# A hybrid diffusion backbone on one core: lent load buffers are taken until the first phase's last load, and the build pictures transfers at 405 GB/s

## The chip, the core and the metric

The kernel runs on one core of a Trainium2 chip. A core has four engines that compute: TensorE (PE in the profile, its weight loads PEld), VectorE (DVE), ScalarE (ACT) and GpSimd (POOL). Each works through its own list of instructions in order, and waits on semaphores for the others. A fifth, SyncE (SP), here only issues transfers (DMA) from the chip's memory (HBM); these transfers, once issued, share 16 DMA engines. The metric is the time of one execution on the device, in microseconds (us).

## The reference, cut to what matters

One trunk layer (D_MODEL 2048) is computed for 128 context tokens and for 128 latent tokens with the same weights; the kernel puts both side by side as 256 columns. Each kind of token has its own shift and scale from a conditioning vector. What the first phase of the kernel covers is the start of `block`:

```python
def block(x, mod, p, lb, s0_hg, s0_gdn, rows):
    shift1, scale1, gate1, shift2, scale2, gate2 = jnp.split(mod, 6, axis=-1)   # mod = silu(c) @ w_mod + b_mod
    h = rmsnorm(x, p['norm1_g']) * (1.0 + scale1) + shift1
    (hq, hi, hgo, hff, hfb, cu, cv, gqkv, ggo, ga, gbeta, gates) = jnp.split(h @ p['w_in'], ...)
    o_a, s_hg = hgrn2_branch(...)        # three branches over the columns of h @ w_in
    o_b = chunk_mlp_branch(...)
    o_c, s_gdn = gdn_branch(...)
    merged = g_a * (o_a @ p['w_br_hg']) + g_b * (o_b @ p['w_br_cm']) + g_c * (o_c @ p['w_br_gdn'])
    x = x + gate1 * (merged @ p['w_out'])
    h2 = rmsnorm(x, p['norm2_g']) * (1.0 + scale2) + shift2
    x = x + gate2 * (jnp.square(jax.nn.relu(h2 @ p['w_ff1'])) @ p['w_ff2'])
```

All arrays are float32. Weights are read once, and nearly all of the 460 MB that move are weights.

## The kernel before, in words

**Units and steps.** The weights come in units of 128 x 1024 float32 (512 KB). `run_stream` (line 393) gets a list of steps, most of them one unit with its matmuls, and emits instructions for all engines while it walks along the list. A normal unit is split first (`split`, line 388): ACT casts it to a rounded copy `wh`, DVE computes the remainder `wl` (a subtraction), and PE then runs three products for each piece (high by high, high by low, low by high), 24 matmuls for a unit in the first phase. A "whole" unit is not split: PE multiplies it as it is.

**The first phase.** It has 88 units, numbered 0 to 87 here. 64 of them are whole: the columns of `w_mod` for shift1 and scale1 (`in_wmods`), eight for each of eight blocks of 256 columns, chain 0 to chain 7. After the eighth unit of a block a short chain of work (`chain` in `start_steps`) turns the sum into shift and scale and applies them to two of the 16 row blocks of h: ACT copies the sum (`m<-pf`), PE transposes it (`pf<-sel,m`), DVE adds the bias (`modc`, `gs`) and scales (`tp`), ACT modulates (`tp<-tp,modc,gs`, four times) and casts (`Hh`), DVE computes `Hl`. The other 24 units are normal ones of `w_in` (`in_win`, `in_winh`), of the forget gates, and are woven in between: the three that use chain n's rows come when chain n is done. At the end stand units 81 and 82 (the last of `w_mod`), 83 (the transposes of chain 7 lie in the middle of its matmuls), 84, and then 85, 86 and 87, which need chain 7. Unit 88 is the first of the second phase, from where all units are normal.

**Load buffers.** Three buffers of one unit (`raw`) serve the whole program. In the first phase twelve more are lent: the halves of six large tiles (`z`) that the program needs only later. SP issues a load when a buffer is free, in the order of the units: a whole unit frees its buffer when PE has multiplied it, a normal one when DVE has subtracted. In `run_stream` a lent buffer is taken up again only while fewer than `last` loads have been issued; before, `last` is `self.lend - len(raws)`, that is 88 - 15 = 73. So loads 0 to 72 may go to any of 15 buffers, later ones to three. The split copies have three pairs of buffers, and two further lent pairs (`z` again) while fewer than 88 loads have been issued.

**The order is written by the build.** Every engine's list comes from a planning clock in the build (`Clock`, `Meter`): each instruction that is emitted is booked at an estimated time. The side work of a phase (chains, normalisations, scans) is written as generators, "fillers"; `pump` lets a filler emit its next piece when by that clock its inputs are ready and DVE and ACT are not ahead by more than a margin. `run_stream` decides in the same way how early a unit is split: not if by that clock its load lands more than 1.5 us after PE's present time. Transfers are booked one behind the other at a fixed rate, 3.6e5 bytes/us (360 GB/s). From the second phase on DVE also computes the remaining columns of `w_mod` as background work (`mods`), with loads of its own (`mraw`).

## Time and profile before

| what | value |
|---|---|
| time, median of 3 runs | 2002.61 us (2000.73 to 2003.5) |
| profiled execution: its time, its span | 2000.7 us, 1998.9 us |
| mean granted TensorE clock | 0.99 |
| PE busy | 1941.3 us, 97% of the span |
| DVE, ACT busy | 1407.2 us (70%), 952.6 us (48%) |
| moved by DMA | 460.51 MB, mean 230 GB/s |
| first matmul of unit 88 | 174.65 us after the span's start |

The span goes from the first to the last instruction; the time has 1.8 us more around it. Matmuls overlap in their pipeline, so a busy PE may still run slowly: how long a unit takes is read from the start of its first matmul to the start of the next unit's. The three products of a normal unit appear as `pb<-Hh,wh`, `pb<-Hh,wl` and `pb<-Hl,wh` (with `z` in place of `wh` and `wl` where the pair of buffers is a lent one); the whole units appear as `pf<-raw,cst` or `pf<-z,cst`, by their load buffer. Line L173 is the helper through which all instructions go, so lines tell nothing and the tiles tell all.

### The profile page before, as it was taken

How to read it: one execution, taken by the hardware profiler on the slowest of the kernel's cores; microseconds unless marked ns; L12 is line 12 of the kernel's file. 1: busy time of each engine (PE TensorE's matmuls, PEld its weight loads, DVE VectorE, ACT ScalarE, POOL GpSimd, SP SyncE). 2: the span in 40 equal slices, each digit the busy share in tenths (PEclk: the TensorE clock that was granted, in tenths of full speed). 3: DMA queues.
4: the chain of work that ended last, by engine and by line, in shares of the span. 5: the costliest groups of instructions: out<-in, count | busy, mean ns of one | idle time of the engine just before them, and what ended most of it. 6: DMA issues, size and time to landing. Idle time of an engine off the chain costs nothing.

```text
span 1998.9 us, 30561 instructions
## 1 busy us (share of the span) xinstructions
PE 1941.3 (97%) x11927; PEld 1707.3 (85%) x11927; DVE 1407.2 (70%) x2064; ACT 952.6 (48%) x1419; POOL 49.0 (2%) x120
## 2 busy tenths in 40 slices
PE   6979999999999999999999999899999999999997
PEld 3758988999888889888887888899988998998886
DVE  2325898989887998856876896766766766555476
ACT  3324646476655545366543445544444443344334
POOL 0000000000000001011000000000000000000000
PEclk9999999999999999999999999999999999999999
DMA  9956667565656866756678786566667666566664
GB/s 374 403 205 225 224 209 248 188 231 190 210 186 230 269 221 228 271 176 202 234 237 308 246 282 211 182 220 225 228 225 250 218 235 230 189 203 210 210 233 148
DMA packets 125216, 460.51 MB, mean 230 GB/s; under 512 B 14416, under 2 KB 14992, under 8 KB 122896
## 3 DMA queue, kind: packets, MB, share of 16 engines
q1 hardware_dynamic: 117072, 423.96, 62.6%
q0 software_dynamic: 7568, 34.35, 5.0%
q8 instruction: 93, 1.52, 0.3%
q14 instruction: 51, 0.42, 0.1%
q10 hardware_dynamic: 432, 0.26, 0.0%
HBM read 447.97 MB, written 10.53 MB: 229 GB/s over the span
## 4 chain that ended last, share of the span: by engine, by line
PE 89%; DMA 4%; DVE 3%; ACT 2%; issue 1%; POOL 0%; ACTq 0%; POOLq 0%; DVEq 0%
PE pb L173 80%; PE pf L173 9%; DVE wl L173 1%; DMA raw<-in_win 1%; DVE z L173 1%; ACT wh L173 1%; DMA raw<-in_wff2c 1%; DMA par<-in_par 1%; DMA z<-in_win 1%; DVE m L173 0%; ACT tp L173 0%; DMA z<-in_wmods 0%; ACT z L173 0%; DMA z<-sp 0%; DMA z<-in_s0gd 0%
## 5 line engine op out<-in xcount | busy, mean ns | idle before, releaser
L173 DVE TENSOR_TENSOR wl<-raw,wh 128x1024 fp32r<-128x1024 f32 x586 | 712.3, 1220 | 442.1 <-ACT wh L173 440.5
L173 ACT CAST wh<-raw 128x1024 fp32r<-128x1024 f32 x586 | 612.5, 1048 | 801.3 <-PE pb L173 677.0
L173 PE MATMUL pb<-Hh,wh 128*128 128x256 f32 (+1 forms) x1856 | 529.1, 288 | 9.3 <-ACT wh L173 8.4
L173 PE MATMUL pb<-Hh,wl 128*128 128x256 f32 (+1 forms) x1856 | 525.5, 286 | 4.3 <-DVE wl L173 4.3
L173 PE MATMUL pb<-Hl,wh 128*128 128x256 f32 (+1 forms) x1856 | 510.7, 285 | 0.0
L173 PE MATMUL pb<-wh,z 128*128 128x512 f32 x1368 | 428.2, 392 | 0.0
L173 PEld LDWEIGHTS pb<-Hh,wh 128*128 128x128 f32 (+1 forms) x1856 | 358.8, 193 | 20.5 <-ACT wh L173 11.3
L173 PEld LDWEIGHTS pb<-Hh,wl 128*128 128x128 f32 (+1 forms) x1856 | 359.0, 193 | 6.3 <-DVE wl L173 6.0
L173 PEld LDWEIGHTS pb<-Hl,wh 128*128 128x128 f32 (+1 forms) x1856 | 350.0, 193 | 0.1
L173 PE MATMUL pb<-wh,Hh 128*128 128x512 f32 (+1 forms) x800 | 315.7, 395 | 0.1
L173 DVE SCALAR_TENSOR_TENSOR junk<-mraw,cb 128x1024 bf16<-128x1024 f32 x256 | 312.0, 1219 | 3.1 <-DMA cb<-csd 1.8
L173 PE MATMUL pb<-wl,Hh 128*128 128x512 f32 (+1 forms) x800 | 306.2, 383 | 1.4 <-DVE wl L173 1.4
L173 PE MATMUL pb<-wh,Hl 128*128 128x512 f32 (+1 forms) x800 | 306.2, 383 | 0.0
L173 PEld LDWEIGHTS pb<-wh,z 128*128 128x128 f32 x1368 | 257.6, 188 | 55.7 <-ACT z L173 0.2
L173 PE MATMUL pb<-wl,z 128*128 128x512 f32 x684 | 268.8, 393 | 2.0 <-DVE wl L173 2.0
L173 PEld LDWEIGHTS pb<-wh,Hl 128*128 128x128 f32 x800 | 151.0, 189 | 29.8
L173 PEld LDWEIGHTS pb<-wl,Hh 128*128 128x128 f32 x800 | 151.4, 189 | 28.1 <-DVE wl L173 2.4
L173 PEld LDWEIGHTS pb<-wh,Hh 128*128 128x128 f32 x800 | 151.3, 189 | 27.4 <-ACT wh L173 0.5
L173 PEld LDWEIGHTS pb<-wl,z 128*128 128x128 f32 x684 | 128.4, 188 | 32.2 <-DVE wl L173 4.1
L173 DVE TENSOR_TENSOR z<-z,z 128x512 f32<-128x512 f32 (+4 forms) x101 | 71.7, 743 | 13.3 <-ACT z L173 12.5
L173 DVE SCALAR_TENSOR_TENSOR cy<-z,par,cy 128x258 f32<-128x258 f32 (+1 forms) x192 | 53.6, 331 | 1.9
L173 PEld LDWEIGHTS pf<-m,z 128*128 128x128 f32 x384 | 49.1, 191 | 3.3 <-ACT z L173 0.4
(189 smaller groups left out, 1276.3 us busy)
## 6 DMA issues: line engine op xcount, KB each, us to landing
raw<-in_win SPq DMA_DIRECT2D x246, 512.0 KB, 4.2
raw<-in_wff SPq DMA_DIRECT2D x224, 512.0 KB, 3.8
mraw<-in_wmodr SPq DMA_DIRECT2D x128, 512.0 KB, 4.8
raw<-in_wbr SPq DMA_DIRECT2D x48, 512.0 KB, 3.8
z<-in_wmods SPq DMA_DIRECT2D x44, 512.0 KB, 10.0
raw<-in_wmods SPq DMA_DIRECT2D x20, 512.0 KB, 7.9
cb<-csd POOLq DMA_DIRECT2D x8, 1024.0 KB, 7.7
raw<-in_wouta SPq DMA_DIRECT2D x16, 512.0 KB, 4.4
```

Of the source, the lines that this page charges most:

```text
L173: return f(*a, **k)
```

## The change

Two edits. A lent buffer is now taken up again as long as fewer than 88 loads have been issued, that is until the last load of the first phase. And the planning clock books a transfer at 4.05e5 bytes/us.

```diff
@@ in Meter.__getattr__, the booking of a transfer
                 size = int(np.prod(outs[0].shape)) * 4
-                clock.dma = max(clock.dma, start + DMA0) + size / 3.6e5
+                clock.dma = max(clock.dma, start + DMA0) + size / 4.05e5
                 clock.mark("dma", rd, wr, clock.dma + DMA1)
@@ in run_stream
         lent = [self.slot(z, [P, 2, NB]) for z in (3, 4, 5, 6, 7, 0)]
         raws = [0, 1, 2] + [t[:, h, :] for t in lent for h in range(2)]
-        last = self.lend - len(raws)
+        last = self.lend
         pairs = [None] * 3 + [8, 9]
```

The work is the same: PE, DVE, POOL and SP have the same number of instructions, ACT two table loads fewer. What moves is the order, and which buffer a load goes to. Three places are shown.

SP's loads from unit 72 on, before (`z_11` to `z_16` are the six lent tiles, each `raw` one of the three standing buffers, `mraw` the first two loads of the background work):

```order
L173 DMA z_16_138<-in_win 128x1024
L173 DMA raw_800<-in_wmods 128x1024
L173 DMA raw_804<-in_wmods 128x1024
L173 DMA raw_859<-in_wmods 128x1024
L173 DMA mraw_891<-in_wmodr 128x1024
L173 DMA mraw_893<-in_wmodr 128x1024
L173 DMA raw_989<-in_winh 128x1024
L173 DMA raw_993<-in_wmods 128x1024
L173 DMA raw_997<-in_wmods 128x1024
L173 DMA raw_1004<-in_wmods 128x1024
L173 DMA raw_1032<-in_win 128x1024
```

and the same place now:

```order
L173 DMA z_16_138<-in_win 128x1024
L173 DMA z_16_138<-in_wmods 128x1024
L173 DMA z_14_136<-in_wmods 128x1024
L173 DMA raw_802<-in_wmods 128x1024
L173 DMA raw_806<-in_winh 128x1024
L173 DMA z_12_134<-in_wmods 128x1024
L173 DMA z_11_133<-in_wmods 128x1024
L173 DMA mraw_861<-in_wmodr 128x1024
L173 DMA mraw_863<-in_wmodr 128x1024
L173 DMA raw_875<-in_wmods 128x1024
L173 DMA z_12_134<-in_win 128x1024
```

Behind unit 72 the loads before went to the three standing buffers in turn; now four of the next seven go to lent ones, and the load of unit 76 (`in_winh`), which stood behind both background loads, stands ahead of them. Units 80 to 87 now all have lent buffers.

ACT's list about chain 5, before (the casts of units 61 and 65, `z_81` and `z_86`, and of unit 69, `wh_865`; `m_84`, `tp_832` and `Hh` are the chain):

```order
L173 CAST z_81_769<-z_16_138 128x1024
L173 COPY m_84_806<-pf_718 96x512
L173 ACTIVATE tp_832<-tp_832,modc,gs 128x128 x4
L173 CAST Hh_191<-tp_832 128x512
L173 CAST z_86_845<-z_12_134 128x1024
L173 COPY tp_851<-pf_849 32x128
L173 CAST wh_865<-z_14_136 128x1024
```

and now (unit 65 is `z_85`, unit 69 `wh_881`):

```order
L173 CAST z_81_769<-z_16_138 128x1024
L173 COPY m_84_808<-pf_718 96x512
L173 CAST z_85_810<-z_12_134 128x1024
L173 COPY tp_849<-pf_847 32x128
L173 ACTIVATE tp_838<-tp_838,modc,gs 128x128 x4
L173 CAST Hh_194<-tp_838 128x512
L173 ACT_TABLE_LOAD
L173 ACTIVATE rshd_870<-rshd_870 128x16
L173 CAST wh_881<-z_14_136 128x1024
```

The cast of unit 65 has moved from behind the chain's modulation to ahead of it, and DVE's subtraction with it.

ACT's list at the end of the first phase, before (the casts of units 76, 80 and 83, then chain 7, then units 84, 85 and 86):

```order
L173 CAST wh_1000<-raw_989 128x1024
L173 CAST z_113_1042<-raw_1032 128x1024
L173 CAST z_115_1071<-raw_1045 128x1024
L173 COPY m_119_1084<-pf_986 96x512
L173 ACTIVATE tp_1104<-tp_1104,modc,gs 128x128 x4
L173 CAST Hh_191<-tp_1104 128x512
L173 CAST wh_1123<-raw_1074 128x1024
L173 CAST wh_1129<-raw_1078 128x1024
L173 CAST wh_1160<-raw_1082 128x1024
```

and now (unit 76 has moved up ahead of chain 6's modulation; then units 80, 83, 84, 85, 86, chain 7, and unit 87):

```order
L173 CAST wh_961<-raw_806 128x1024
L173 ACTIVATE tp_991<-tp_991,modc,gs 128x128 x4
L173 CAST Hh_194<-tp_991 128x512
L173 CAST z_108_1013<-z_12_134 128x1024
L173 CAST z_109_1045<-z_13_135 128x1024
L173 CAST wh_1052<-z_16_138 128x1024
L173 CAST wh_1080<-z_11_133 128x1024
L173 CAST wh_1086<-z_15_137 128x1024
L173 COPY m_117_1092<-pf_999 96x512
L173 ACTIVATE tp_1118<-tp_1118,modc,gs 128x128 x4
L173 CAST Hh_194<-tp_1118 128x512
L173 CAST wh_1156<-z_15_137 128x1024
```

The casts of units 84, 85 and 86 have moved from behind chain 7 to ahead of it. PE's list holds the units in the same order as before. In the second phase and the branches behind it most of the fillers' pieces stand earlier among PE's unit matmuls, by 20 to 220 matmuls of 128 x 256 and some by up to 366, and some stand later, by up to 192; from the first of the two large products of the channel sub-layer on, PE's list is the same again.

## The prediction

> **What bounds the kernel now.** First the page's slices: PE is at nine tenths or more nearly everywhere, so the time is PE's work plus the few places where PE waits. Two of the early slices stand out.

> ```profile
> PE   6979999999999999999999999899999999999997
> DMA  9956667565656866756678786566667666566664
> ```

> Slices are 50 us; the third and fourth (100 to 200 us) have the DMA engines half idle, and still PE shows a 7. The table of busy times by stretches of 10 us shows it closer (the last three columns are granted clock, DMA share, GB/s):

> ```profile
> 80.00:90.00 10.00, 10.00 (x75) 6.62 (x72) 2.96 (x3) 3.78 (x7) 0.00 (x0) 1.00 1.03 409
> 120.00:130.00 10.00, 10.00 (x73) 7.43 (x76) 1.02 (x4) 2.11 (x5) 0.00 (x0) 1.00 0.29 105
> 130.00:140.00 10.00, 5.41 (x26) 4.43 (x21) 1.92 (x2) 1.78 (x3) 0.00 (x0) 0.72 0.61 211
> 160.00:170.00 10.00, 8.67 (x58) 8.47 (x59) 6.54 (x6) 4.39 (x5) 0.00 (x0) 0.83 0.63 184
> 170.00:180.00 10.00, 10.00 (x87) 10.00 (x86) 3.91 (x4) 7.25 (x10) 0.00 (x0) 1.00 0.52 165
> ```

> Until 90 us transfers run at 409 GB/s, a unit in 1.28 us. Then they fall to a quarter, although the first phase still lacks 15 units, and right behind it PE is idle half of the time and its clock falls to 0.72. The timeline of SP's queue (start, duration, count) says what the loads wait for:

> ```profile
> 102.18 0.33 SPq L173 DMA_DIRECT2D z<-in_win  x1
> 106.25 7.06 SPq L173 DMA_DIRECT2D raw<-in_wmods  x3
> 129.86 0.33 SPq L173 DMA_DIRECT2D raw<-in_winh  x1
> 142.17 0.33 SPq L173 DMA_DIRECT2D raw<-in_win  x1
> ```

> At 102.18 unit 72 goes out, the last into a lent buffer. Units 73 to 75 follow as PE frees the three standing buffers, and unit 76 goes out only at 129.86, when PE multiplies unit 73. The chain that ended last (start, duration, what) runs through exactly these loads:

> ```profile
> 118.14 1.85 PE pf L173 x12
> 119.99 3.07 PE pb L173 x24
> 123.06 1.83 PE pf L173 x8
> 124.89 1.62 PE pb L173 x12
> 126.52 0.79 PE pf L173 x8
> 127.30 1.53 PE pb L173 x12
> 128.84 1.01 PE pf L173 x5
> ...
> 129.86 3.61 DMA raw<-in_winh
> ...
> 133.50 1.05 ACT wh L173
> ...
> 134.58 1.24 DVE wl L173
> ...
> 135.85 5.27 PE pb L173 x23
> 141.13 1.03 PE pf L173 x5
> ...
> 148.01 4.48 PE pb L173 x23
> ...
> 154.32 0.90 PE pb L173 x6
> 155.22 0.84 PE pf L173 x8
> ...
> 158.84 0.62 ACT Hh L173
> ...
> 161.71 70.64 PE pb L173 x575
> ...
> 233.25 2.87 PE pb L173 x24
> ```

> Undisturbed, three whole units take 1.85 us, two take 1.83, a normal unit 3.07, one with a chain's transposes in its middle 1.62 + 0.79 + 1.53 = 3.94, and a normal unit that follows another 2.87.

> **The change part by part.** It adds no work. The removed time is read as start to start, against those paces, at four units; the clock's slow restart is in it. The ends of the first and the last stretch are in PE's timeline:

> ```profile
> 112.36 0.60 PE L173 MATMUL pf<-z,cst 128*32 128x512 f32 x2
> 113.88 0.38 PE L173 MATMUL pb<-Hh,z 128*128 128x256 f32 x1 [0.92 <-ACT z L173]
> 160.46 0.38 PE L173 MATMUL pb<-Hh,wh 128*128 128x256 f32 x1 [2.17 <-ACT wh L173]
> 174.65 0.39 PE L173 MATMUL pb<-Hh,z 128*128 128x256 f32 x2
> ```

> Unit 65 (PE free at 112.96, next whole units at 118.14): 118.14 - 112.96 - 3.07 = 2.11. Its load had long landed; its cast stood behind chain 5's modulation on ACT.
> Unit 76: (141.13 - 128.84) - 1.85 - 3.07 = 7.37. It waits for a load that could not be issued: 3.61 for the transfer, then cast 1.05 and subtraction 1.24.
> Unit 80, the same way: next whole units start at 148.01 + 4.48 = 152.49, so (152.49 - 141.13) - 1.85 - 3.07 = 6.44.
> Units 84 to 87: unit 83 should end at 154.32 + 3.94 = 158.26, unit 88 starts at 174.65: 174.65 - 158.26 - 4 x 2.87 = 4.91. Here the wait is ACT's: the cast of unit 84 stands behind chain 7, whose Hh ends at 158.84 + 0.62.
> Together 2.11 + 7.37 + 6.44 + 4.91 = 20.83 us.

> Do all four go? I lay PE's list out from 112.96 with the paces above. Unit 65's cast is now ahead of the modulation, right behind the chain's copy, which before ran at 107.10:

> ```profile
> 107.10 0.58 ACT L173 COPY m<-pf 96x512 f32<-96x512 f32 x1 [7.70 <-PE pf L173]
> 114.95 1.28 ACT L173 ACT_TABLE_LOAD   x1
> 162.71 0.68 DVE L173 TENSOR_TENSOR Hl<-tp,Hh 128x512 fp32r<-128x512 f32 x1
> ```

> It is split by 107.68 + 1.05 + 1.24 = 110, before PE wants it at 112.96. Then unit 69 starts at 117.9, 72 at 122.8, the whole units 73 to 75 at 126.7, unit 76 at 128.6, 80 at 133.5, 83 at 138.4, 84 at 142.3, 85 at 145.2, 86 at 148.1, 87 at 150.9 and 88 at 153.8: 20.8 us earlier than 174.65, the same sum.
> The loads: 73 and 74 go out right behind 72 at about 102; 75 and 76 at about 106 and 107, as units 59 and 60 free the standing buffers; the last one, 87, takes the buffer of unit 71, free at 122.8, and lands by 122.8 + 3.6 = 126.4, some 19 us before its cast. Units 88 to 90 use the standing buffers of 76, 75 and 79, free at 125.7, 128.6 and 133.5, again 10 us or more ahead. So one transfer could be several times slower and cost nothing.
> The splits: unit 69's cast now stands behind chain 5 and a table load. ACT's modulation starts about 111.6, after the copy of a transpose that PE does at 111.1; then 1.66 + 0.62 + 1.28 + 0.2 + 1.05 gives a cast by 116.4, wl by 117.6, Hl by 118.3 (0.68). PE reaches its third matmul, the first with Hl, at about 118.2: a loss of 0 to 0.2. Unit 76: its cast waits for chain 6's copy, which PE's whole units free at 122.8; split by 125.7, wanted at 128.6. Units 83 to 86 are split by 137, well ahead.
> The tightest place is chain 7: its transposes end at 138.4 + 1.62 + 0.79 = 140.8. From there to the end of Hh took 159.46 - 156.06 = 3.4 in the chain above, and Hl 0.7 more: 144.9. Unit 85 wants it at 145.2. I take 0; were it missed, the price is a few tenths, bounded by the 4.91 that the place costs now.
> The two lent pairs of split buffers are used last for units 80 and 83, so 84 to 90 turn over three pairs: unit 89's split waits for 86 to end (151.0) and for the four evictions behind it (2.07 together), and is done by 155.5 where PE wants it at 155.3. A loss of 0.2.

> ```profile
> 173.59 2.07 ACT L173 ACTIVATE z<-pb 128x512 f32<-128x512 f32 x4
> ```

> Behind unit 88, PE has the same matmuls, and everything shifts. What the new order of the fillers does there can't be read from before; it is bounded by the rows there are. The waits of PE behind 200 us (total, times, longest), and a stretch in which PE is busy but its clock is low, where tiny matmuls of the fillers stand close together:

> ```profile
> PE pb L173 <- DVE wl L173: 4.4, 10, 0.8
> PE pf L173 <- DVE tp L173: 4.2, 1, 4.2
> PE pf L173 <- DMA z<-sp: 2.2, 1, 2.2
> 590.00:595.00 5.00, 5.00 (x29) 4.63 (x29) 4.25 (x11) 0.89 (x3) 0.00 (x0) 0.67 0.82 300
> 595.00:600.00 5.00, 5.00 (x16) 3.97 (x15) 3.26 (x5) 2.55 (x3) 0.00 (x0) 0.65 0.21 61
> ```

> Best case: the low clock (about 5 x 0.33 + 5 x 0.35 = 3.4) and the spill wait (2.2) go: -5.6. Worst plausible: another wait like the longest, 4.2, with a slow restart like unit 76's (5.27 for 23 matmuls against 23/24 of 3.07, 2.3): +6.5. I take 0, since most pieces keep their neighbours and PE's waits there are few.

> Sum: 2000.7 - 20.8 + 0.4 = 1980.3 for the profiled execution's time. The median of the runs is 1.9 above that execution, so I predict 1982.2.

> **The rivals.** *A: the early casts block ACT.* Engines take their lists in order; ACT now has casts of later units ahead of chains 5, 6 and 7. If one waits for its load or its buffer, the chain behind it is late, and PE stands at units 69, 80 or 85 instead of 65 and 84. Then the loads' terms are gained and the other two are not: 2000.7 - 7.37 - 6.44 = 1986.9, 1988.8 by the median. For it: only 0.3 us lie between chain 7 and unit 85. Against it: every load of the layout lands 10 us ahead. [...]

> *B: the order behind the phase costs more than the phase gives.* Fillers now stand up to 366 matmuls, 366 x 0.12 = 44 us, earlier in PE's list; PE, in order, waits wherever DVE, ACT or a spill's reload is not that much earlier too. At 6.5 us for each such wait with its slow restart, four of them take 26 and the time is 2002.6 - 20.8 + 26 = 2007.8; it is slower than before from the fourth on. For it: DVE is the busiest engine behind PE, and ten small waits for wl are there already. Against it: the chains start earlier by the same reason, and the trace has only two waits above 1 us.

> *C: the change does not do what it says.* The refilled buffers might be held just as long, if SP, in order, stood at one of them. Then 2000 to 2003. For it only that SP has one list; against it, that the buffers of units 56, 57, 59 and 60 are free before 108.

> *D: more is gained*: forecast and best case behind, 2002.6 - 20.4 - 5.6 = 1976.6.

> **How the numbers follow.** Forecast 1982.2 with what lies within 3.5 of it, 66%; A and smaller mixtures between 1986 and 1991, 16%; D 8%; B 6%, of which a part only eats up the gain; C 4%. The range 1976 to 1991 takes in forecast, A and D. A difference of 0.2% (4 us) is about what a measurement of this kernel can tell from none. Faster by more than that: forecast, A, D and a part of B, 0.92; within it 0.04; slower 0.04.

> **What would show it.** Right: in the changed profile DMA stays above 300 GB/s to about 125 us; SP's loads of units 73 to 76 start between 102 and 108; no idle PE of over 0.5 us between 113 and 155 and a clock of 1.00 there; unit 88's first matmul at about 154. Wrong: PE waiting for ACT Hh or DVE Hl at unit 69 or 85 (A), new waits above 2 us between 200 and 900 (B), a first matmul of unit 88 beyond 160 (A or C). If unit 88 starts at 154 and the time is above 1988, the loss is behind the phase, and the step that took 0 for it is wrong.

## The result: 13 us of the 22 that the first phase gave

The changed kernel takes 1987.12 us in the median of five runs (1984.75 to 1992.67), against 2000.73 for the kernel before on the same chip (five runs, 1999.47 to 2003.5): a ratio of 0.9931 with a 95% interval of 0.9913 to 0.995. The forecast was 1982.2. The profiled execution took 1987.7 us, its span is 1985.9 instead of 1998.9.

### The profile after, in the first phase

The slices of the page, 50 us each, no longer show the dip in the third:

```profile
PE   6999999999999999998999999999999999999997
DMA  9977575756576867555768776566667666666664
```

The busy times by stretches of 10 us (PE, PEld, DVE, ACT, POOL, granted clock, DMA share, GB/s) and SP's queue (start, duration) show why:

```profile
110.00:120.00 10.00, 10.00 (x78) 6.72 (x73) 3.69 (x8) 5.47 (x9) 1.07 (x2) 1.00 1.00 358
120.00:130.00 10.00, 10.00 (x73) 7.25 (x69) 3.82 (x7) 6.16 (x10) 0.00 (x0) 1.00 1.02 411
130.00:140.00 10.00, 10.00 (x73) 6.95 (x73) 5.25 (x8) 3.36 (x4) 0.00 (x0) 1.00 0.52 203
```

```profile
101.06 0.86 SPq L173 DMA_DIRECT2D z<-in_wmods  x2
104.71 0.33 SPq L173 DMA_DIRECT2D raw<-in_wmods  x1
105.55 0.33 SPq L173 DMA_DIRECT2D raw<-in_winh  x1
...
123.28 0.33 SPq L173 DMA_DIRECT2D z<-in_winh  x1
```

Transfers run at 358 to 411 GB/s up to 130 us (before: 105 between 120 and 130). Units 73 and 74 go out at 101, 75 at 104.7, unit 76 (`in_winh`) at 105.55 instead of 129.86, and the last load of the phase, unit 87, at 123.28. Between 110 and 140 us PE is never idle, at full clock. The chain that ended last is PE alone here:

```profile
111.42 3.04 PE pb L173 x24
114.46 1.85 PE pf L173 x12
...
125.17 1.85 PE pf L173 x12
127.02 3.06 PE pb L173 x24
130.08 1.85 PE pf L173 x12
131.93 3.06 PE pb L173 x24
134.99 1.83 PE pf L173 x8
...
138.43 0.79 PE pf L173 x8
139.22 20.85 PE pb L173 x173
```

Unit 65 is multiplied from 111.42 without a gap, unit 76 begins at 127.02, unit 80 at 131.93, and chain 7's transposes (138.43) no longer stop what follows: 173 matmuls stand in one piece. By the count of matmuls the first of unit 88 stands at 152.1, 22.5 us earlier than before.

### The profile after, behind the first phase

To see what is left of the 22.5 us, the program is cut at two instructions that both kernels have: DVE's 41st and 261st subtraction of a unit, early in the second phase and behind the branches. Before they start at 216.2 and 989.7, after at 193.7 and 975.4. One row of the busy times covers that whole stretch; first the kernel before, then the changed one:

```profile
216.20:989.70 773.50, 768.20 (x4778) 686.70 (x4777) 649.88 (x1129) 433.76 (x786) 35.88 (x92) 1.00 0.66 218
```

```profile
193.70:975.40 781.70, 769.08 (x4778) 686.49 (x4778) 652.17 (x1129) 433.25 (x785) 35.91 (x92) 1.00 0.64 216
```

The same 4778 matmuls take 781.7 instead of 773.5 us, 8.2 more. PE's idle time is 781.7 - 769.1 = 12.6 against 5.3: 7.3 of the 8.2. The waits of PE between 700 and 1000 us (total, times, longest) name it:

```profile
PE pb L173 <- ACT z L173: 4.1, 1, 4.1
PE pf L173 <- DMA z<-in_s0gd: 3.1, 1, 3.1
...
PE pf L173 <- DMA z<-sp: 0.7, 1, 0.7
```

and of the kernel before, between 720 and 1020:

```profile
PE pf L173 <- DMA z<-sp: 2.2, 1, 2.2
...
PE pf L173 <- DMA z<-in_s0gd: 0.7, 2, 0.5
```

The wait for a reload from the spill shrank, and two new waits came: 3.1 us for the load of the gated delta branch's initial state (`in_s0gd`) and 4.1 us for a cast of ACT. In PE's timeline after:

```profile
744.55 1.74 PE L173 MATMUL pf<-z,z 128*128 128x128 f32 x8 [3.07 <-DMA z<-in_s0gd]
...
915.73 1.13 PE L173 MATMUL pf<-tp,z 128*128 128x128 f32 x8
917.49 1.16 PE L173 MATMUL pf<-tp,z 128*128 128x128 f32 x8 [0.63 <-DVE z L173]
922.72 0.80 PE L173 MATMUL pb<-wh,z 128*128 128x512 f32 x1 [4.07 <-ACT z L173]
```

The second is at the product of the chunk MLP branch with its output weights. Its inputs are the chunk MLP's sums (`pf<-tp,z`, 32 small matmuls; the last 16 are shown here), which then pass DVE (scale, gate) and ACT (the cast, 920.49). In the changed list the last sums stand right in front of the product, 4 us ahead of it; before there were 29 us between them:

```profile
906.65 1.05 PE L173 MATMUL pf<-tp,z 128*128 128x128 f32 x8
...
936.62 0.48 PE L173 MATMUL pb<-wh,z 128*128 128x512 f32 x1
```

So 22.5 us are won up to the second phase, 8.2 given back up to 975, and another 1.3 by the end: 13.0. The experiments ask which edit does which, and whether the two new waits are the loss.

### The profile page after: what moved, and what is told of

Same layout as the page of the kernel before. It is cut to its first block, busy times and chain, and to the rows that moved or that the text cites. A ratio compares the mean times of both kernels' runs of the same rounds, so it can differ in the third digit from the quotient of the medians.

```text
span 1985.9 us, 30577 instructions
## 1 busy us (share of the span) xinstructions
PE 1934.0 (97%) x11927; PEld 1700.7 (86%) x11927; DVE 1409.0 (71%) x2064; ACT 950.7 (48%) x1417; POOL 49.0 (2%) x120
## 4 chain that ended last, share of the span: by engine, by line
PE 83%; DVE 8%; DMA 5%; ACT 2%; issue 2%; POOL 0%; ACTq 0%; DVEq 0%; POOLq 0%
PE pb L173 75%; PE pf L173 9%; DVE wl L173 3%; DVE z L173 2%; ACT wh L173 1%; DMA raw<-in_win 1%; DVE junk L173 1%; DVE m L173 1%; ACT z L173 1%; DMA par<-in_par 1%; DMA z<-in_win 1%; DMA raw<-in_wbr 0%; DMA raw<-in_wff2c 0%; DMA z<-in_wmods 0%; DMA raw<-in_wff2a 0%
## 5 line engine op out<-in xcount | busy, mean ns | idle before, releaser
L173 DVE TENSOR_TENSOR wl<-raw,wh 128x1024 fp32r<-128x1024 f32 x584 | 709.8, 1221 | 437.0 <-ACT wh L173 435.4
L173 ACT CAST wh<-raw 128x1024 fp32r<-128x1024 f32 x584 | 611.2, 1048 | 796.2 <-PE pb L173 638.6
L173 PE MATMUL pb<-Hh,wh 128*128 128x256 f32 x1872 | 532.2, 287 | 3.7 <-ACT wh L173 2.3
L173 PE MATMUL pb<-Hh,wl 128*128 128x256 f32 x1872 | 527.6, 284 | 2.0 <-DVE wl L173 2.0
L173 PE MATMUL pb<-Hl,wh 128*128 128x256 f32 x1872 | 513.7, 284 | 0.0
L173 PE MATMUL pb<-wh,z 128*128 128x512 f32 x1368 | 429.4, 393 | 4.1 <-ACT z L173 4.1
L173 PEld LDWEIGHTS pb<-Hh,wh 128*128 128x128 f32 x1872 | 360.0, 192 | 14.9 <-issue 5.0
L173 PEld LDWEIGHTS pb<-Hh,wl 128*128 128x128 f32 x1872 | 360.2, 192 | 3.1 <-DVE wl L173 2.8
L173 PEld LDWEIGHTS pb<-Hl,wh 128*128 128x128 f32 x1872 | 351.4, 192 | 0.1
L173 PE MATMUL pb<-wh,Hh 128*128 128x512 f32 (+1 forms) x800 | 313.7, 392 | 0.0
L173 DVE SCALAR_TENSOR_TENSOR junk<-mraw,cb 128x1024 bf16<-128x1024 f32 x256 | 312.4, 1220 | 1.8 <-DMA mraw<-in_wmodr 0.3
L173 PEld LDWEIGHTS pb<-wh,z 128*128 128x128 f32 x1368 | 258.2, 189 | 60.5 <-ACT z L173 4.3
L173 PE MATMUL pb<-wl,Hh 128*128 128x512 f32 (+1 forms) x800 | 305.7, 382 | 1.7 <-DVE wl L173 1.7
L173 PE MATMUL pb<-wh,Hl 128*128 128x512 f32 (+1 forms) x800 | 305.2, 381 | 0.0
L173 PE MATMUL pb<-wl,z 128*128 128x512 f32 x684 | 269.5, 394 | 4.1 <-DVE wl L173 4.1
L173 PEld LDWEIGHTS pb<-wl,Hh 128*128 128x128 f32 x800 | 150.8, 189 | 29.5 <-DVE wl L173 4.0
L173 PEld LDWEIGHTS pb<-wh,Hl 128*128 128x128 f32 x800 | 150.5, 188 | 29.1
L173 PEld LDWEIGHTS pb<-wh,Hh 128*128 128x128 f32 x800 | 150.7, 188 | 27.1
L173 PEld LDWEIGHTS pb<-wl,z 128*128 128x128 f32 x684 | 128.8, 188 | 34.8 <-DVE wl L173 6.8
L173 DVE TENSOR_TENSOR z<-z,z 128x512 f32<-128x512 f32 (+4 forms) x103 | 74.0, 754 | 20.0 <-ACT z L173 19.1
L173 DVE SCALAR_TENSOR_TENSOR cy<-z,par,cy 128x258 f32<-128x258 f32 (+1 forms) x192 | 53.7, 332 | 1.9
L173 ACT ACTIVATE z<-pb 128x512 f32<-128x512 f32 x88 | 48.3, 599 | 5.5 <-PE pb L173 3.0
```

The lines of the kernel that those rows point to most:

```text
L173: return f(*a, **k)
```

## The experiments

All times below stand against runs of the kernel before on the same chip (medians 1998.56 to 2000.73). For each, "front" is the start of DVE's 41st subtraction in the profiled execution, and "behind" the span from there to the end; before they are 216.2 and 1782.7, in the changed kernel 193.7 and 1792.2.

Two theories. **T**: both edits together give the first phase's gain, and the rate edit loses some of it, because it rewrites the order of the fillers behind the phase. **R**: the order there costs nothing; the second phase, starting 20 us earlier, runs into new collisions whatever the order.

### The buffers alone

```diff
-        last = self.lend - len(raws)
+        last = self.lend
```

> The buffer edit alone: a lent buffer is taken until the last load of the first phase, the planning clock stays at 360 GB/s. The computation is the same. In the first phase the cast of unit 65 stays behind chain 5 and those of units 85 and 86 behind chain 7; behind the phase every engine has the list of before. Theory T (the faster clock's new order of the fillers behind the phase lost 8 to 10 us of a first-phase gain of 22): the loads' gain and most of the casts' gain come (22 - 2.1 for unit 65 - about 2 at unit 85 = 18 us) and nothing is lost behind, so 2000.7 - 18 = 1982 to 1984 us, ratio about 0.991, the one wait for a spill of 2.2 us still there and no other new wait above 2.5 us between 700 and 960. Theory R (the loss comes because the second phase starts some 20 us earlier, whatever the order): the same 18 us in front, 8 lost behind, 1990 to 1992 us.

1983.01 us, ratio 0.9918 (0.9905 to 0.9932); front 199.0, behind 1778.9. Its median is below that of both edits together, though the two intervals overlap. Behind the phase nothing is lost although the stretch begins 17 us earlier: R falls. (Its profiled execution is even 3.8 us shorter there than that of the kernel before, with the same lists: the low clock at 591 us, worth 3.4, does not occur in it.) In front it lacks two terms. Unit 65 still loses its 2.1 us, and at unit 85, whose cast is behind chain 7 again, PE waits for its split and for the chain's `Hl`:

```profile
147.19 0.39 PE L173 MATMUL pb<-Hh,wl 128*128 128x256 f32 x1 [0.88 <-DVE wl L173]
148.93 0.38 PE L173 MATMUL pb<-Hl,wh 128*128 128x256 f32 x1 [1.35 <-DVE Hl L173]
```

### The rate alone

```diff
-                clock.dma = max(clock.dma, start + DMA0) + size / 3.6e5
+                clock.dma = max(clock.dma, start + DMA0) + size / 4.05e5
```

> The rate edit alone: transfers are booked at 405 GB/s, lent buffers are given up at load 73 as before. The computation is the same. The first phase has nearly the order of before (the cast of unit 65 goes ahead of the chain), behind the phase every engine has the list of the changed kernel. Theory T: a gain of about 2 us at unit 65 and a loss of 8 to 10 behind the phase, 2000.7 - 2 + 8 to 10 = 2007 to 2009 us, ratio 1.003 to 1.004, and waits of about 3 us for a state load and 4 us ahead of the branch's product between 740 and 945, as in the changed kernel. Theory R: the order behind the phase costs nothing by itself, 1998 to 2000 us.

2008.54 us, ratio 1.0039 (1.0027 to 1.0051): slower than before. Front 213.8 (2.4 us gained, of which unit 65 is 2.1), behind 1792.9 (10.2 lost). Over the whole second phase and the rest PE has the same two waits, with the first phase as slow as before:

```profile
PE pb L173 <- ACT z L173: 4.1, 1, 4.1
...
PE pf L173 <- DMA z<-in_s0gd: 2.7, 1, 2.7
```

So the loss hangs on the order, not on when the stretch starts.

### Both edits, the slower rate again behind the phase

```diff
+        self.rate = 4.05e5
...
-                clock.dma = max(clock.dma, start + DMA0) + size / 4.05e5
+                clock.dma = max(clock.dma, start + DMA0) + size / clock.rate
...
                 st["dma"] += 1
+                if st["dma"] == self.lend:
+                    self.clock.rate = 3.6e5
```

> Both edits, but the planning clock goes back to 360 GB/s once the first phase's 88 loads are issued. The computation is the same. In the first phase every engine has the list of the changed kernel, behind it that of before. Theory T: the whole 22 us of the first phase and nothing lost behind, 2000.7 - 22 = 1978 to 1980 us, ratio 0.989, some 8 us below the changed kernel. Theory R: 1986 to 1988 us, as the changed kernel.

1977.21 us, ratio 0.9884 (0.9871 to 0.9896), 10 us under the changed kernel and the lowest median of all; front 192.4, behind 1783.6. The waits between 700 and 1000 us are those of the kernel before:

```profile
PE pf L174 <- DMA z<-sp: 2.1, 2, 1.8
...
PE pf L174 <- DMA z<-in_s0gd: 1.1, 3, 0.6
```

T is confirmed with its size: the rate edit's order costs 9 to 10 us behind the phase (1792.2 against 1783.6 here, 1792.9 against 1782.7 with the rate alone).

### Other rates behind the phase

Is a faster pictured rate worse as such? The kernel just shown, with 320 or 380 GB/s in place of 360 behind the phase.

> Both edits, the planning clock at 405 GB/s in the first phase and at 320 GB/s behind it. The computation is the same; the first phase is that of the changed kernel. If a faster pictured rate costs steadily (pieces stand earlier in PE's list the faster it is), this is at or below the 1977.2 us of the kernel with 360 behind: 1973 to 1977 us. If what counts is only how single pieces happen to fall, it lies anywhere within 1973 to 1985 us, without a trend over 320, 360, 380 and 405.

> Both edits, the planning clock at 405 GB/s in the first phase and at 380 GB/s behind it. The computation is the same; the first phase is that of the changed kernel. If a faster pictured rate costs steadily: between 1977.2 us (360) and 1987.1 us (405), about 1981 to 1983 us. If single pieces decide: anywhere within 1974 to 1990 us, with waits at other places than the two of the changed kernel.

320 GB/s: 1981.1 us, ratio 0.9913 (0.99 to 0.9926), behind 1786.8. 380 GB/s: 1990.41 us, ratio 0.9954 (0.9937 to 0.9971), behind 1794.8. With 360 and 405 the order is 1981, 1977, 1990, 1987: no steady trend. The times do fall into two groups, and the group is told by the same two waits, which the kernel with 380 has as well (those with 320 and 360 have neither):

```profile
PE pb L174 <- ACT z L174: 4.1, 1, 4.1
PE pf L174 <- DMA z<-in_s0gd: 2.8, 1, 2.8
```

The expectation for 380 GB/s was wrong in this: it said waits at other places than the two of the changed kernel. What the kernel with 320 loses behind the phase against the one with 360 (1786.8 against 1783.6) is not a wait: PE idles 5.6 us there between the two cuts, less than the 6.5 with 360, but its clock is at half for 13.7 us in this execution (0.74 between 560 and 580 us, 0.76 between 690 and 697) instead of 6.8.

### The first wait: the state load

POOL issues four transfers in one go, reload, state, reload, state; PE needs the state first. In the changed kernel, the two state loads between 730 and 750 us took this long from issue to landing (KB each, median us):

```profile
z<-in_s0gd POOLq DMA_DIRECT2D x2, 256.0 KB, 9.2
```

and before, between 765 and 785 us:

```profile
z<-in_s0gd POOLq DMA_DIRECT2D x2, 256.0 KB, 6.3
```

PE asks for the state at nearly the same distance: 5.2 us after its issue in the changed kernel (741.48 - 736.32), 5.6 before (776.36 - 770.80). What differs is the landing of this first load, 8.1 us after its issue instead of 5.9. The loads beside it are slower too (the two reloads take 8.5 us instead of 5.8 in the median, six loads of `in_win` 6.5 instead of 4.8); why they are was not followed.

The experiment turns each pair round in the changed kernel:

```diff
-        nc.gpsimd.dma_start(z[:, 0:1024], self.spill[s * 4 + hp])
         ...
         nc.gpsimd.dma_start(L, self.I["s0gd"][:, :, 2 * hp:2 * hp + 2, :])
+        nc.gpsimd.dma_start(z[:, 0:1024], self.spill[s * 4 + hp])
```

> The changed kernel with one swap on POOL: in the gated delta branch the load of the initial state is issued ahead of the reload of the spilled tile, instead of behind it; every other engine's list is that of the changed kernel. The computation is the same. If the 3.07 us wait for that state load at 741 us and the slow clock behind it (1.7 us) come from the load's late issue on POOL, they go or shrink and the time falls by 2 to 5 us to 1982 to 1985 us; the reload's own wait may grow by up to 1 us. If the transfer is late whatever its place in the queue (the 7 us from issue to landing set it), the wait stays above 2 us and the time is that of the changed kernel, 1987 us.

1983.18 us, ratio 0.9913 (0.9901 to 0.9926), 4 us under the changed kernel; behind 1787.8 instead of 1792.2. The two intervals overlap, so it is the wait in the trace that carries this reading. The two state loads land after 6.7 us in the median, the wait is 0.4, and the other new wait stands as it was:

```profile
PE pb L173 <- ACT z L173: 4.1, 1, 4.1
PE pf L173 <- DMA z<-sp: 0.9, 1, 0.9
...
PE pf L173 <- DMA z<-in_s0gd: 0.4, 1, 0.4
```

Is the swap simply good? The same swap in the kernel with 360 GB/s behind the phase:

> The kernel with both edits and the planning clock back at 360 GB/s behind the first phase, and besides on POOL the load of the gated delta branch's initial state issued ahead of the reload of the spilled tile. The computation is the same. In that kernel the waits for the state loads are 1.1 us together and those for the reloads 2.1. If the place in POOL's queue sets them, the first go and the second grow by up to 1: 1976 to 1978 us, not to be told from 1977.2. A theory by which the swap is a gain of its own, whatever the order (about 4 us, as in the changed kernel): 1973 us.

1978.9 us, ratio 0.9898 (0.9884 to 0.9912), not to be told from 1977.2. Its wait for the state falls from 1.1 to 0.2 us, but there was no more to win: the swap is worth 4 us only in the order in which the state lands later than PE asks for it.

### The second wait: not DVE's load

In the changed kernel DVE is busy without a pause from 899 to 920 us, right ahead of the product, with some of its background work (`junk`) among it. The experiment cuts four of these operations short and leaves every list as it is.

```diff
+            if clock.small and name == "scalar_tensor_tensor":
+                k = dict(k, **{x: k[x][:, :1] for x in ("out", "in0", "in1")})
             return f(*a, **k)
...
+                self.clock.small = m in (66, 67)
                 nc.vector.scalar_tensor_tensor(out=junk, ...)
+                self.clock.small = False
```

> The changed kernel, with four operations of DVE's background work (those at 897 to 917 us in the trace of the changed kernel) cut to an eighth of their columns, so that an eighth only of these sums is computed; every list of instructions is that of the changed kernel. It takes about 4 x 1.0 us of work from DVE ahead of the branch's product at 918.65, where PE waits 4.07 us for a cast of ACT that waits for DVE. If DVE's load there makes the wait: it falls to under 1.5 us, the slow clock at 922 goes, and the time falls by 3 to 5 us to 1982 to 1984 us. If the wait comes from elsewhere (PE's own late sums in front of DVE's chain): it stays above 3 us and the time is 1987.

1986.0 us, ratio 0.993 (0.9918 to 0.9942), as the changed kernel; and the wait is longer, not shorter:

```profile
916.59 2.02 PE L176 MATMUL pf<-tp,z 128*128 128x128 f32 x16
923.13 0.65 PE L176 MATMUL pb<-wh,z 128*128 128x512 f32 x1 [4.52 <-ACT z L176]
```

The theory that DVE's load makes the wait is refuted. With DVE relieved, PE runs its 16 sums in one piece, and then nothing stands in its list between them and the product that needs them. What it waits for is the way there and back: sums, DVE, ACT's cast.

### The second wait: the place in PE's list

In the changed kernel both later reloads of the gated delta branch stand ahead of all loads of the chunk MLP (`in_wsT`) in POOL's list, and the last of those goes out at 905.57, 17 us ahead of the product:

```profile
844.65 0.55 POOL L173 DMA_DIRECT2D z<-sp  x1
...
905.57 0.54 POOL L173 DMA_DIRECT2D tp<-in_wsT  x1 [1.78 <-PE pb L173]
```

before, the last reload came behind them:

```profile
903.23 0.54 POOL L173 DMA_DIRECT2D tp<-in_wsT  x1 [2.52 <-PE pb L173]
908.10 0.65 POOL L173 DMA_DIRECT2D z<-sp  x1
```

So the swapped kernel gets one more edit: while the chunk MLP's pieces live, no piece of another filler is emitted except the background's.

```diff
             for g in list(self.fillers):
+                if self.alone not in (None, g) and self.alone not in self.dead and g not in self.kids and g is not self.background:
+                    continue
...
-            self.before["B"] = self.add(self.gmlp(), first=True)
+            self.before["B"] = self.alone = self.add(self.gmlp(), first=True)
```

> The changed kernel with the swap on POOL, and besides the pieces of the gated delta branch held back in the lists while the pieces of the chunk MLP live. The computation is the same; the lists differ from the swapped kernel only between about 880 and 980 us. PE's sums of the chunk MLP then stand 58 rows ahead of the product that needs them instead of 1 (133 rows with the order of before). If the gated delta pieces ahead of them made them late: the 4.1 us wait for ACT's cast and the slow clock behind it go, and with both places mended the changed kernel's order costs what the order of before costs: 1983.2 - 5 = 1977 to 1979 us, as the kernel with 360 GB/s behind the first phase. If something else makes them late (their own loads, PE's order of units), a wait of 2 us or more stays there, or the held pieces make a new one ahead of the last branch's product: 1981 to 1985 us.

1979.5 us, ratio 0.9894 (0.9876 to 0.9911), half a us above what was expected; behind 1782.5, as before the change (1782.7). The sums end at 903.8, 13 us ahead of the product, which waits for nothing:

```profile
902.78 1.05 PE L173 MATMUL pf<-tp,z 128*128 128x128 f32 x8
...
916.60 0.39 PE L173 MATMUL pb<-wh,z 128*128 128x512 f32 x1
```

With both places mended the order that 405 GB/s writes costs no more than the order of before: the stretch between the two cuts takes 773.5 us (197.0 to 970.5), as before the change. The two waits and what hung on them were the loss. The sum is the same, but not the parts: PE still idles 8.1 us there against 5.3, and the half clock at 591 us, which cost the kernel before 3.4, is missing.

The place of the reloads on POOL is not the cause by itself. They stand ahead of all `in_wsT` loads here too (the last at 845.15, the first `in_wsT` at 877.95), and with 320 GB/s behind the phase (858.81 and 868.15), and neither kernel has the wait. What goes with it is the time from the end of the last sums to the product: 4 us in the changed kernel, 13 here, 26 with 320, 29 before.

## Why the prediction was right, and which step failed

The forecast was 1982.2, the range 1976 to 1991, the chance of faster 0.92; the time is 1987.12. The range holds it, but one part of the sum was right almost to the tenth and another wrong by 9 us. That the range holds it is luck in part: it reached up to 1991 to take in rival A, which did not happen.

**The four terms of the first phase: right.** Read the same way, from the starts of the whole units in the two chains: unit 65, from PE free to the next whole unit, 118.14 - 112.96 = 5.18 before and 114.46 - 111.42 = 3.04 after, so 2.14 (forecast 2.11). Unit 76, (141.13 - 128.84) - (130.08 - 125.17) = 7.38 (7.37). Unit 80, (152.49 - 141.13) - (134.99 - 130.08) = 6.45 (6.44). Units 84 to 87, (174.65 - 152.49) - (152.1 - 134.99) = 5.05 (4.91). Together 21.0; forecast 20.8 less 0.4. The two losses of 0.2 at units 69 and 89 did not come. Which edit earns which is also shown: the buffers alone bring the two terms of the loads and 2.0 of the last one, the rate alone brings unit 65. The other 3 us of the last term need both.

**Unit 88 at 153.8: 1.7 too late,** by what the sum did not hold: in the changed kernel's execution PE was 1.54 us ahead already when it came to unit 65 (111.42 against 112.96), from the clock near 50 us. That belongs to the execution and not to the change (last section).

**"I take 0" for the new order behind the phase: wrong.** It was said that most pieces keep their neighbours and that PE's waits there are few. The number of matmuls by which a piece moves was not the point: the sums of the chunk MLP lost their distance to the product that they feed, and the first load of the state met PE's demand at the old distance but took 8.1 us instead of 5.9. The stretch lost 8.2 us by the two cuts and the profiled execution 9.5 by its end, outside the bounds of -5.6 to +6.5, whose upper end allowed for one new wait and not for two. This step is the whole miss: the profiled execution lies 7.4 above its forecast (1987.7 against 1980.3), which is 9.5 less the 2.1 that the first phase gave beyond the forecast 20.4. The median misses by 4.9 only: the forecast put it 1.9 above the profiled execution, as in the first three runs of the kernel before, and it came 0.6 below. The sign that had been named for it (unit 88 at 154, the time above 1988) is nearly what came: 152.1 and 1987.12.

**Its best case came too, and was outweighed.** The reload's wait fell from 2.2 to 0.7, and the low clock at 591 us, where tiny matmuls stand close together, is gone in the changed kernel. But the clock was low for as long in all, 6.8 us, in two shorter pieces behind the new waits (they show in the next fence): no net gain.

```profile
740.00:750.00 10.00, 6.93 (x46) 6.76 (x45) 7.28 (x13) 1.04 (x1) 0.00 (x0) 0.83 0.99 360
920.00:930.00 10.00, 7.28 (x25) 5.67 (x26) 4.92 (x7) 7.52 (x12) 0.00 (x0) 0.83 0.00 0
```

**The rivals.** A (early casts block ACT) did not happen: no wait at unit 69 or 85, and DMA, SP and clock show what was forecast. C is refuted by the loads of units 73 to 76. B is what happened, in a smaller size: two waits, of 3.1 and 4.1 us, each followed in this execution by 3.4 us of half clock, which is 1.7 lost. That is 4.8 and 5.8 us instead of 6.5 each, and two instead of the four that would have made the kernel slower. With the rate alone B decides the sign. D, 1976.6, is about what the kernel with 360 GB/s behind the phase reaches, though not for D's reasons: its gain behind is nothing, and the low clock is there again.

**What stays open.** Why the planning clock at 380 or 405 GB/s puts the last sums of the chunk MLP right in front of their product, and at 320 or 360 not, was not followed through its bookings. The 1.3 us that the changed kernel loses between 975 us and its end were not tried; kernels with the same lists there differ by about as much.

## What to carry to other kernels

An edit of a number that a planner uses is two edits: what it does where it was meant to act, and a new draw of the order everywhere else. Cost the second by looking, for every product that consumes a filler's result, at how many matmuls still stand between the last piece and that product; here a distance that fell to nothing was a wait of 4 us, whatever the average shift. And try the number in the phase that needs it alone: here that was worth 10 us more than the change.

## What the runs showed of the hardware that was not expected

**The same short waits drop the clock in one execution and not in the other.** Near 48 us every execution has two waits of PE, 1.02 us for a cast and 0.88 for a subtraction. The kernel before, between 45 and 55 us, has a granted clock of 0.83,

```profile
45.00:55.00 10.00, 8.10 (x48) 5.14 (x48) 4.19 (x4) 4.86 (x8) 0.00 (x0) 0.83 1.02 409
```

and the changed kernel, with the same waits, 1.00:

```profile
45.00:55.00 10.00, 8.10 (x58) 4.84 (x53) 4.19 (x4) 4.66 (x7) 0.00 (x0) 1.00 1.03 410
```

So do kernels with the same list there: the one with 360 GB/s behind the phase has 1.00, the last one above 0.83. The piece of half clock in the kernel before lasts 3.41 us (48.97 to 52.38, clock 0.50) and costs 1.7 (0.83 over 10 us is 1.7 lost). Together with what happens before 30 us (between 18 and 30 us PE gets through 49 matmuls in the last kernel above, 64 to 67 in the others) this spreads "front" from 192.0 to 197.0 among the executions with the changed kernel's first phase, and is why differences of 2 us between these kernels are not read as effects.

The length of a wait alone does not tell it: the kernel with DVE relieved has 3.0 us of the wait for the state load, and its clock between 740 and 750 us is 1.00, where the changed kernel, with 3.07, has 0.83. Why was not shown.

**The truer rate wrote the worse order.** Loads ran at 409 GB/s between 80 and 90 us in the kernel before and at 411 between 120 and 130 in the changed one, so 405 is nearly what the first phase does, and it writes the better order there; behind it, 360 wrote the better one.
